# A two-layer attention and convolution kernel: the adaLN products placed anew in a hand-written order, and two norms that keep the squares of their last two tiles apart

## The chip, the cores and the metric

The kernel runs as one program on one NeuronCore of a Trainium2 chip. The metric is the device time of one execution in microseconds (us); lower is better.

## The reference, cut to what matters

Two layers work on 512 latent tokens of 1024 features. Layer 0 is a chunked gated linear attention (GLA) that also reads 256 context tokens; layer 1 is a Conformer convolution module. Each is followed by a SwiGLU feed-forward network (FFN), and each of the four sub-layers has an RMSNorm ahead of it that is scaled and shifted by a modulation (adaLN):

```
mod_lat = jax.nn.silu(c) @ w_mod[i] + b_mod[i]          # 6 vectors of 1024 for each layer
sh1, sc1, gt1, sh2, sc2, gt2 = jnp.split(mod_lat, 6)
h = modulate(rmsnorm(x, norm_mix_g[i]), sh1, sc1)       # y*(1+scale)+shift
x = x + gt1 * mixer(h)
x = x + gt2 * swiglu(modulate(rmsnorm(x, norm_ffn_g[i]), sh2, sc2), ...)
out = rmsnorm(x, final_norm_g)
```

`w_mod[i]` is a 1024 x 6144 matrix for each layer. An RMSNorm needs, for each token, the sum of the squares of its 1024 features.

## The kernel before, in words

Tokens lie along the free dimension and features along the 128 partitions, so the residual stream x is eight tiles `xs[0..7]` of 128 x 512. All projections run on TensorE (PE) as three matmuls on high and low parts of each number (`mm3`, lines 95 to 97; lines 369 to 371 for the values). The weights come by DMA from SyncE's queue (SP) into `wr`, ScalarE (ACT) casts them to a high part `wh` (L110), and VectorE (DVE) or GpSimd (POOL) subtracts to get the low part `wl` (L111).

The modulation vectors are not matmuls. `mod_jobs` (L217 to L238) is a generator: each step multiplies one 128 x 1024 tile of `w_mod` with the broadcast silu(c) on DVE and adds along the row ("product", L231), and only then asks for the DMA of the next tile (L223), because the tile `wm` has one buffer. `step(n)` takes n steps. The first step only loads. Products 1 to 24 (columns 16 to 39 of layer 0) are taken in the attention stage; `ffn(0, ...)` takes the later ones, two for each pair of hidden tiles.

The attention stage lies in a `manual_schedule` block: on PE, ACT, DVE and POOL the instructions run in the order in which the program writes them. That order is `plan` (L768): a list of projections ("fills"), and behind each the small stages that are run after it, by letters: `a` loads and splits coming weights, `o` copies the fill's result out, `m` is one product, `D`/`d` the decays of a head, `J`/`I` the masked scores (J scales queries and keys on DVE, L433/L434; I multiplies them on PE, L443), `X`/`y`/`x` the decays and transposes of the context's keys (y ends with L472 on DVE, x is L484 on PE), `S`, `K`, `T` states (T is L548 on DVE), `O`, `P`, `B`, `b` a head's output: O its matmuls (L560 to L562) and products with the gate (L573), P its mean square (L158 on PE, then eight small DVE operations L164 to L190), B the broadcast of the result on PE (L170), b its use (L586 to L590). `w304` and the like are parts of the output projection.

The plan holds 21 letters `m`; the line behind it takes the three that are left:

```
step(24 - sum(s_.split().count("m") for _, s_ in plan))
```

Outside the block a planner orders the instructions: it may take an instruction that comes later in the program into a time in which it believes the engine free. SP's order is always the planner's.

After the plan come the output projection `out_proj("wgo", ...)` in two token halves for its last two tiles (6 and 7), and `Norm.bc`. `Norm(7)` squares tiles 0 to 6 on ACT (L886) and adds them up on POOL (L888) in one accumulator; the square of tile 7 (L893) stays apart. Then `rstd_y` sums over the features with matmuls against a column of ones (L158), once for each of the two parts and each of two blocks of 128 tokens. There are four such norms: n1 behind the attention, n2 behind the first FFN, n3 behind the convolution, n4 at the end.

Of the kernel before, what the change touches and what calls it, by code (L numbers as in the profile page):

```python
# [55 lines left out]
def hybrid_kernel(ctx: ExitStack, tc: tile.TileContext, t: dict):  # L56
# [93 lines left out]
    def col(c, n=1):  # L150
        return cols[:, c:c + n]
# [62 lines left out]
    def make_a(dst, sc, g):  # L214
        dve.scalar_tensor_tensor(dst, sc, 1.0, g, op0=ALU.add, op1=ALU.mult)
# [378 lines left out]
    with tc.manual_schedule(engines=ENGS):  # L594
# [140 lines left out]
        d3 = dsum[:, 32:64].rearrange("p (k i two) -> p i k two", i=2, two=2)  # L735
# [8 lines left out]
        for k in range(KC):  # L744
            o = slice(k % 2 * CTX, (k % 2 + 1) * CTX)
# [3 lines left out]
        for k in range(KC + 1):  # L749
# [5 lines left out]
            if prev:  # L755
# [9 lines left out]

        plan = (("k2", "a D0 o d0 m"), ("g0", "o a"), ("kc0", "a o"), ("kc1", "o J0 a m"),  # L768
# [7 lines left out]
        names = [f for f, _ in plan] + ["w0", "w1", "w2", "w3"]  # L776
        head, parts = {}, {}

# [197 lines left out]
            nx.add(m, xs[m], c0, c1)  # L976
        return f

    n1, n2, n3, n4 = Norm(7), Norm(7), Norm(7), Norm(7)
    make_a(acol[:, 16:24], mod[0][:, 32:40], col(C_GFFN, 8))  # L980
    in1 = SubIn(n1, acol[:, 16:24], mod[0][:, 24:32])
    out_proj("wgo", KC, og, closing(mod[0][:, 16:24], n1), 6, in1, done={m: head[m][0] for m in head})
# [24 lines left out]
    D0, D7, A0, S1, S2, B7, G7 = 14, 13, 6, 12, 4, 20, 20  # L1007
# [550 lines left out]
```

## Time and profile before

| what | value |
|---|---|
| median of 3 runs | 1269.54 us (1267.61 to 1273.08) |
| the profiled execution's own time | 1270.32 us |
| its span from the first to the last instruction | 1268.5 us |
| mean granted TensorE clock | 0.984 of full speed |
| TensorE busy | 1231.4 us, 97% of the span |
| VectorE busy | 721.6 us, 57% |
| products on tile wm | 72 of 1206 to 3331 ns, median 1225 |

All stretches and starting times are microseconds from the start of the span. "Idle before" in a row of the timeline stands in brackets, with what ended it. The granted clock is 1.00 at 2.4 GHz and 0.50 at 1.2 GHz.

### The profile page before, as it was taken

The page shows a single profiled execution, that of the slowest core. Times are in us where ns is not written, and L with a number is a line of the kernel's source. Part 1 is how long each engine was busy: PE and PEld are TensorE (multiplying, and loading weights), DVE is VectorE, ACT ScalarE, POOL GpSimd, SP SyncE. Part 2 cuts the span into 40 slices and gives each one's busy share as a digit, 9 for nine tenths or more (in the row PEclk, how much of TensorE's full clock was granted, in tenths as well). Part 3 has the DMA queues.
Part 4 walks back from the last instruction along what each step waited for, and adds up shares of the span by engine and source line. Part 5 has one row for each costly group of instructions (what it writes and reads, how often), then busy time and mean ns, then how long its engine had stood idle before and what let it go on. Part 6 is the DMA issues. An engine that isn't in the chain of part 4 may idle for free.

```text
span 1268.5 us, 17022 instructions
## 1 busy us (share of the span) xinstructions
PE 1231.4 (97%) x6692; PEld 1068.6 (84%) x6692; DVE 721.6 (57%) x1289; ACT 476.1 (38%) x748; POOL 192.5 (15%) x154
## 2 busy tenths in 40 slices
PE   8899899999899999999999999999999999999997
PEld 7678799898798888888888988989988888888886
DVE  2997986755775555555323679986744333332223
ACT  3245655433342222222222469745522222232220
POOL 0033211112300000000011169913000000000110
PEclk7999999999899999999999999999999999999999
DMA  7742442323545656556333274422254333333322
GB/s 277 230 134 72 141 150 82 106 90 117 167 151 195 191 184 198 193 188 207 105 103 97 67 249 152 139 61 74 84 166 150 100 100 100 100 91 91 99 67 67
DMA packets 57780, 169.18 MB, mean 133 GB/s; under 512 B 6498, under 2 KB 12386, under 8 KB 57700
## 3 DMA queue, kind: packets, MB, share of 16 engines
q1 hardware_dynamic: 56036, 166.00, 40.8%
q10 hardware_dynamic: 1664, 2.10, 0.5%
q8 instruction: 52, 0.85, 0.3%
q14 instruction: 28, 0.23, 0.1%
HBM read 164.67 MB, written 3.41 MB: 132 GB/s over the span
## 4 chain that ended last, share of the span: by engine, by line
PE 77%; DVE 14%; issue 4%; ACT 3%; DMA 1%; POOL 1%; DVEq 0%; ACTq 0%; POOLq 0%
PE pm L95 22%; PE pm L96 22%; PE pm L97 22%; DVE g L256 3%; DVE pa L1096 2%; DVE wl L111 2%; PE pm L370 1%; PE pm L369 1%; PE pm L371 1%; DMA wm<-wmod 1%; ACT wh L110 1%; PE pa L623 1%; PE pm L530 1%; DVE pm L1096 1%; DVE t L276 1%
## 5 line engine op out<-in xcount | busy, mean ns | idle before, releaser
L110 ACT CAST wh<-wr 128x1024 fp32r<-128x1024 f32 (+2 forms) x197 | 200.4, 1025 | 484.1 <-PE pm L96 470.4
L97 PE MATMUL pm<-h,wl 128*128 128x512 f32 (+1 forms) x1008 | 372.0, 370 | 1.9 <-POOL wl L111 1.9
L96 PE MATMUL pm<-h,wh 128*128 128x512 f32 (+1 forms) x1008 | 371.0, 370 | 0.4 <-DVE h L199 0.4
L95 PE MATMUL pm<-h,wh 128*128 128x512 f32 (+1 forms) x1008 | 371.1, 371 | 0.2 <-ACT wh L110 0.2
L111 DVE TENSOR_TENSOR wl<-wr,wh 128x1024 fp32r<-128x1024 f32 (+1 forms) x176 | 221.1, 1260 | 244.7 <-ACT wh L110 242.8
L97 PEld LDWEIGHTS pm<-h,wl 128*128 128x128 f32 x1008 | 190.2, 189 | 35.1 <-POOL wl L111 2.8
L96 PEld LDWEIGHTS pm<-h,wh 128*128 128x128 f32 x1008 | 190.2, 189 | 32.2 <-DVE h L199 0.6
L95 PEld LDWEIGHTS pm<-h,wh 128*128 128x128 f32 x1008 | 189.3, 189 | 32.1 <-ACT wh L110 0.7
L95 PE MATMUL pm<-s,wh 128*128 128x512 f32 (+1 forms) x540 | 186.9, 346 | 1.1 <-ACT s L1276 1.1
L96 PE MATMUL pm<-s,wh 128*128 128x512 f32 (+1 forms) x540 | 186.0, 345 | 0.3 <-DVE s L281 0.2
L97 PE MATMUL pm<-s,wl 128*128 128x512 f32 (+1 forms) x540 | 185.5, 343 | 0.0
L231 DVE SCALAR_TENSOR_TENSOR wm<-wm,sil 128x1024 f32<-128x1024 f32 x72 | 93.9, 1304 | 108.4 <-DMA wm<-wmod 108.2
L888 POOL TENSOR_TENSOR g<-g,g 128x512 f32<-128x512 f32 (+1 forms) x31 | 39.9, 1288 | 748.3 <-ACT g L886 747.7
L96 PEld LDWEIGHTS pm<-s,wh 128*128 128x128 f32 x540 | 103.1, 191 | 13.2 <-DVE s L281 0.9
L95 PEld LDWEIGHTS pm<-s,wh 128*128 128x128 f32 x540 | 103.0, 191 | 13.1 <-ACT s L1276 1.3
L97 PEld LDWEIGHTS pm<-s,wl 128*128 128x128 f32 x540 | 102.9, 191 | 12.0
L111 POOL TENSOR_TENSOR wl<-wr,wh 128x1024 fp32r<-128x1024 f32 x21 | 52.6, 2517 | 215.4 <-ACT wh L110 200.6
L901 DVE SCALAR_TENSOR_TENSOR x<-pm,mod,x 128x256 f32<-128x256 f32 (+1 forms) x44 | 25.7, 600 | 52.6 <-PE pm L97 52.6
L1096 DVE SCALAR_TENSOR_TENSOR pa<-s,cols,pa 128x503 f32<-128x503 f32 (+18 forms) x80 | 52.8, 702 | 0.6
L369 PE MATMUL pm<-wh,h 128*128 128x256 f32 x128 | 37.0, 289 | 0.0
L371 PE MATMUL pm<-wl,h 128*128 128x256 f32 x128 | 36.2, 283 | 0.0
L370 PE MATMUL pm<-wh,h 128*128 128x256 f32 x128 | 36.2, 283 | 0.0
(267 smaller groups left out, 1511.2 us busy)
## 6 DMA issues: line engine op xcount, KB each, us to landing
wr<-wf SPq DMA_DIRECT2D x88, 512.0 KB, 4.3
wm<-wmod SPq DMA_DIRECT2D x72, 512.0 KB, 3.7
wr<-wo SPq DMA_DIRECT2D x32, 512.0 KB, 3.5
wr<-wp SPq DMA_DIRECT2D x24, 512.0 KB, 3.5
s<-toep SPq DMA_DIRECT2D x27, 256.0 KB, 5.4
s<-wmod SPq DMA_DIRECT2D x24, 256.0 KB, 5.1
wr<-wv SPq DMA_DIRECT2D x12, 512.0 KB, 3.8
wr<-wo SPq DMA_DIRECT2D x16, 384.0 KB, 3.2
```

Of the source, the lines that this page charges most:

```text
L95: pe.matmul(out, wh, xh, start=start, stop=False)
L96: pe.matmul(out, wh, xl, start=False, stop=False)
L97: pe.matmul(out, wl, xh, start=False, stop=stop)
L110: act.copy(hi[:, :n], raw[:, :n])
L111: lo_eng.tensor_tensor(lo[:, :n], raw[:, :n], hi[:, :n].bitcast(F32), op=ALU.subtract)
L231: dve.scalar_tensor_tensor(raw, raw, 1.0, sil, op0=ALU.mult, op1=ALU.mult, accum_out=dots[:, o:o + 1])
L256: dve.scalar_tensor_tensor(junk, wt, 1.0, vec, op0=ALU.mult, op1=ALU.mult, accum_out=dsum[:, o:o + 1])
L369: pe.matmul(o, a, wh[:, w], start=k == 0, stop=False)
L370: pe.matmul(o, b, wh[:, w], start=False, stop=False)
L371: pe.matmul(o, a, wl[:, w], start=False, stop=k == KC - 1)
L888: pool.tensor_tensor(self.acc[:, c0:c1], self.acc[:, c0:c1], s[:, c0:c1], op=ALU.add)
L1096: dve.scalar_tensor_tensor(p_[:, lo:hi], u_sb[m][:, lo + s:hi + s], wcol(m, j), p_[:, lo:hi], op0=ALU.mult, op1=ALU.add)
```

## The change

The plan gets three more letters `m`, 24 in all, so that the step behind it takes none. Four letters leave kc1, kc2, kc3 and vc2; seven are added at g0, kc0, vc1, va1, r6, vb3 and r7. The letters that stay keep their place among the other stages. Norms n1 and n3 become `Norm(6)`: the squares of tiles 6 and 7 both stay apart, and POOL no longer adds tile 6.

```diff
-        plan = (("k2", "a D0 o d0 m"), ("g0", "o a"), ("kc0", "a o"), ("kc1", "o J0 a m"),
-                ("k3", "a o Xa0 ya0"), ("kc2", "o a I0 m"), ("kc3", "a o Xa1 xa0 ya1 m"),
-                ("vc3", "a Xb0 o a xa1 yb0"), ("vc2", "xb0 m Xb1 o yb1 m a"), ("vc0", "o a xb1 D1 d1 m"),
-                ("va0", "o J1 S0 S3 K0 m"), ("vb0", "a o S2 I1 m"), ("vc1", "a o a T0 K1 m"),
-                ("va1", "o a D2 d2 S1 m"), ("vb1", "o J2 a O0 T1 m"), ("va2", "o a P0 m D3 O1 d3 J3"),
-                ("vb2", "o a I2 P1 m"), ("r5", "o a B0 K2 b0 B1 b1 m"), ("r6", "o a T2 I3 m"),
-                ("va3", "o a O2 K3 m a m"), ("vb3", "o P2 T3 m"),
-                ("r7", "o a B2 b2 w004 O3 m w104 P3 w204 B3 b3 m w304 w046 w146 w246 w346 w068 w168 w368 w268"))
+        plan = (("k2", "a D0 o d0 m"), ("g0", "o a m"), ("kc0", "a o m"), ("kc1", "o J0 a"),
+                ("k3", "a o Xa0 ya0"), ("kc2", "o a I0"), ("kc3", "a o Xa1 xa0 ya1"),
+                ("vc3", "a Xb0 o a xa1 yb0"), ("vc2", "xb0 Xb1 o yb1 m a"), ("vc0", "o a xb1 D1 d1 m"),
+                ("va0", "o J1 S0 S3 K0 m"), ("vb0", "a o S2 I1 m"), ("vc1", "a o a m T0 K1 m"),
+                ("va1", "o a m D2 d2 S1 m"), ("vb1", "o J2 a O0 T1 m"), ("va2", "o a P0 m D3 O1 d3 J3"),
+                ("vb2", "o a I2 P1 m"), ("r5", "o a B0 K2 b0 B1 b1 m"), ("r6", "o a m T2 I3 m"),
+                ("va3", "o a O2 K3 m a m"), ("vb3", "o m P2 T3 m"),
+                ("r7", "o a B2 b2 m w004 O3 m w104 P3 w204 B3 b3 m w304 w046 w146 w246 w346 w068 w168 w368 w268"))
...
-    n1, n2, n3, n4 = Norm(7), Norm(7), Norm(7), Norm(7)
+    n1, n2, n3, n4 = Norm(6), Norm(7), Norm(6), Norm(7)
```

## Rows read from the trace of the kernel before

**Rows 1.** The page: busy time of each engine, and the chain that ended last

```profile
PE 1231.4 (97%) x6692; PEld 1068.6 (84%) x6692; DVE 721.6 (57%) x1289; ACT 476.1 (38%) x748; POOL 192.5 (15%) x154
...
PE 77%; DVE 14%; issue 4%; ACT 3%; DMA 1%; POOL 1%; DVEq 0%; ACTq 0%; POOLq 0%
```

**Rows 2.** Waits of PE from 110 to 365: total us, times, longest

```profile
PE pm L484 <- DVE g L472: 3.6, 3, 1.5
PE pa L158 <- POOL g L888: 3.1, 2, 2.3
PE pm L170 <- DVE sm L190: 2.5, 1, 2.5
...
PE pa L158 <- ACT g L893: 0.9, 1, 0.9
```

**Rows 3.** Timeline of DVE from 112 to 245: start, duration, instruction, idle before

```profile
130.62 1.22 DVE L231 SCALAR_TENSOR_TENSOR wm<-wm,sil 128x1024 f32<-128x1024 f32 x1
...
136.61 0.68 DVE L434 TENSOR_TENSOR s<-s,s 128x512 f32<-128x512 f32 x1
...
151.96 3.33 DVE L231 SCALAR_TENSOR_TENSOR wm<-wm,sil 128x1024 f32<-128x1024 f32 x1 [0.72 <-DMA wm<-wmod]
```

**Rows 4.** Timeline of PE from 132 to 160

```profile
135.88 1.06 PE L443 MATMUL pa<-s,s 128*128 128x128 f32 x8
137.34 1.16 PE L443 MATMUL pa<-s,s 128*128 128x128 f32 x8 [0.40 <-DVE s L434]
...
158.96 1.01 PE L484 MATMUL pm<-ident,g 128*128 128x128 f32 x4 [1.48 <-DVE g L472]
```

**Rows 5.** Timeline of POOL from 100 to 420

```profile
133.68 2.46 POOL L111 TENSOR_TENSOR wl<-wr,wh 128x1024 fp32r<-128x1024 f32 x1 [9.53 <-ACT wh L110]
...
151.79 2.41 POOL L111 TENSOR_TENSOR wl<-wr,wh 128x1024 fp32r<-128x1024 f32 x1 [5.82 <-ACT wh L110]
...
297.38 1.29 POOL L574 TENSOR_TENSOR g<-g,g 128x512 f32<-128x512 f32 x1 [0.59 <-ACT g L570]
```

**Rows 6.** The tile wm over the whole span: its DMA from issue to landing

```profile
DMA to landing us min/median/max: 3.4/3.7/5.0
```

**Rows 7.** Windows: busy us of PE, PEld, DVE, ACT, POOL, clock, DMA share, GB/s

```profile
160.00:164.00 4.00, 4.00 (x23) 4.00 (x23) 2.73 (x9) 2.95 (x8) 0.00 (x0) 0.57 0.58 216
...
165.00:246.00 81.00, 81.00 (x617) 78.05 (x615) 57.03 (x126) 44.86 (x82) 15.68 (x7) 1.00 0.31 98
...
249.00:252.00 3.00, 3.00 (x12) 2.70 (x11) 2.32 (x5) 0.62 (x1) 0.00 (x0) 0.50 0.44 96
...
256.00:299.00 43.00, 43.00 (x305) 40.39 (x304) 23.36 (x45) 17.54 (x33) 12.66 (x6) 1.00 0.33 105
...
340.00:344.00 4.00, 4.00 (x20) 4.00 (x21) 1.30 (x8) 0.00 (x0) 0.00 (x0) 0.50 0.27 109
```

**Rows 8.** Timeline of DVE from 245 to 362

```profile
259.91 1.65 DVE L548 SCALAR_TENSOR_TENSOR t<-t,dec,pm 128x256 f32<-128x256 f32 x4
...
279.01 1.23 DVE L231 SCALAR_TENSOR_TENSOR wm<-wm,sil 128x1024 f32<-128x1024 f32 x1 [3.47 <-DMA wm<-wmod]
...
297.26 1.40 DVE L573 SCALAR_TENSOR_TENSOR d<-d,cols,pm 128x512 f32<-128x512 f32 x2
...
301.61 0.16 DVE L190 SCALAR_TENSOR_TENSOR sm<-sm,sm 128x4 f32<-128x4 f32 x1
...
331.52 1.23 DVE L231 SCALAR_TENSOR_TENSOR wm<-wm,sil 128x1024 f32<-128x1024 f32 x1 [2.00 <-DMA wm<-wmod]
```

**Rows 9.** Timeline of PE, from 245 to 304 and from 874 to 900

```profile
267.24 0.39 PE L562 MATMUL pm<-s,s 128*128 128x128 f32 x2
...
302.91 1.05 PE L170 MATMUL pm<-ident,sm 128*128 128x128 f32 x8
...
892.80 0.38 PE L158 MATMUL pa<-ones,g 128*128 128x1 f32 x2 [0.80 <-POOL g L888]
...
896.49 0.73 PE L158 MATMUL pa<-ones,g 128*128 128x1 f32 x6
```

## The prediction, on record before the changed kernel ran

> **What bounds the kernel now.** The page comes first: PE is busy for 97% of the span and holds 77% of the chain that ended last, DVE 14% [rows 1]. So an edit on DVE counts only where PE stands and waits for DVE, or where such a wait lowers PE's clock. The waits of PE in the attention stage and just behind it are therefore the second view. There are few: 3.6 us in three waits of the context's transposes for L472, 3.1 us and 0.9 us for the squares of norm n1, 2.5 us for a broadcast [rows 2]. The third view is the timeline around each. What the reader is to see there is that a product is seldom dear by its 1.2 us, but by what it waits for: the next tile is asked for only when the last product is done. A tile takes 3.7 us from issue to landing at the median, 3.4 to 5.0 [rows 6], and a product placed right behind another found its engine idle for 3.47 us [rows 8]. I call that the turnaround: 3.65 us of wait and 1.2 us of work. Everything queued behind a waiting product on DVE waits too.
>
> The fourth view is the granted clock. After waits of 1.5 and 1.48 us near 151 and 159, the stretch 160 to 164 ran at 0.57; after the 2.5 us wait that ended at 248.6, 249 to 252 ran at 0.50; after the waits of norm n1, 340 to 344 ran at 0.50, the lower of the two levels [rows 2, 4, 7]. A wait of about 2 us therefore costs about 1.5 us more: half of the 3 us that the row at 0.50 shows.
>
> **The front of the plan: g0 and kc0 take a product each; kc1, kc2, kc3 and vc2 lose one.** Before, product 1 runs at 130.62, then the gate's subtraction L287, and then J0, whose last operation ends at 137.29 [rows 3]. J0 feeds the two groups of L443 on PE: PE came to the first at 135.88 without a wait and to the second at 137.34 after 0.40 us [rows 4]. In the new order products 2 and 3 stand between L287 and J0.
>
> Product 2's tile is asked for at 131.85 and lands near 135.5. POOL has a subtraction from 133.68 to 136.14 [rows 5], and where product 4 met such a one (151.79 to 154.20) it ran 3.33 us, until 1.1 us behind POOL's end [rows 3, 5]; so product 2 ends at 136.14 + 1.1 = 137.25. Product 3's tile is asked for then: wait 3.7, work 1.15, end 142.1. J0's four operations at 0.61 end at 144.55. The second group of L443 moves from 137.34 to 144.65: PE is late by 7.3 us.
>
> What comes back: the products that left kc1, kc2 and kc3 make the three waits for L472 go away, 3.6 us [rows 2], since DVE, free of three products (one of them 3.33 us long behind a wait of 0.72 [rows 3]), reaches each L472 before a PE that is late by 7 us. The low clock of 160 to 164 goes with them: 0.43 of 4 us, 1.7 us [rows 7]. New is a low clock behind the wait of 7.5 us at 135.9: 1.2 to 2.8 us, by how much of the following 3 to 6 us runs at 0.50; I take 2.0. Sum: 7.3 - 3.6 - 1.7 + 2.0 = +4.0 us, with ends +2.0 (no new low clock) and +4.8. PE is busy for 81.00 of the 81 us from 165 to 246 [rows 7], so nothing there gives it back; the wait at 248.6 is on a chain that starts from PE and moves along.
>
> The Trainium skill (DMA: Bandwidth & Descriptors, Anatomy of one DMA) gives a transfer a fixed part of about 2.0 us and the rest at 436 GB/s; by that the 512 KB tile would take an estimated 3.2 us, and the front would cost 0.9 us less over its two tiles. The trace's 3.4 at the least speaks for the longer one. The Trainium skill (SBUF — State Buffer, Who interferes with whom) says that GpSimd and a VectorE instruction with two SBUF inputs exclude each other for the whole instruction; the 3.33 us product agrees.
>
> **The middle.** vc1 and va1 take a product each. PE is the bound there, and DVE works 57.03 of 81 us [rows 7] and stands idle ahead of both next stages, until PE or ACT has their inputs; the products end inside that idleness: nothing. Without it each would cost its 1.2 us. In r6 product 16 follows 15 directly, so T2, whose last four operations start at 259.91, comes 4.9 us later and ends near 266.6; the ACT scaling behind it ends by 267.1, and PE's first use is L562 at 267.24 [rows 8, 9]: 0 to 0.3 us, I take 0. If PE came there earlier, it would wait for all the rest.
>
> **vb3 and r7.** vb3's new product is a third in a row behind the one at 279.01, so P2 and T3 come 5 us later. PE has the fill of r7 between, 24 matmuls, and was busy for all 43 us from 256 to 299 [rows 7]; its next broadcast still comes behind P2's end, by about 1 us, so I take 0. r7's new product 22 stands behind b2, ahead of O3's two L573 at 297.26 [rows 8]; its tile is there. But product 23 follows those 1.4 us later, where its own old place had a landed tile: 297.3 + 1.2 for product 22, 3.65 for the tile with L573 inside it, 1.15 for product 23, so P3's small operations start at 303.4 and end at 304.9, in place of 301.77 [rows 8]. If POOL's L574 at 297.38 [rows 5] gets ahead of product 22, it is 1.3 us more. PE reaches B3 at 302.91 [rows 9]: a wait of 2.0 to 3.3 us that was not there, and with 0 to 1.7 us of low clock behind it 2.0 to 5.0; I take 4.2, since the wait is like the one at 248.6.
>
> **The three products that stood behind the plan.** They cost PE nothing where they stood: from 256 on PE has no wait [rows 7] until n1. What hurts is later. The product at 331.52, behind 2.00 us of idleness for its tile [rows 8], and a like one 5.6 us later belong to the FFN; the planner took them ahead, and they hold up the subtraction of the residual tiles 5 and 7. That is the 2.3 + 0.9 us of waits for n1's squares [rows 2] and the low clock to 344 [rows 7], half of the 6 us from 338: 6.2 together. The planner takes the next products as soon as a tile is free, so with the three gone it will take others into the same gaps: I take 0, with ends of -6.2 (none ahead of tiles 5 and 7) and +2 (one more late tile).
>
> **The norms.** POOL's adds of tile 6 go: PE waited for them 0.8 us at n1's second half (3.1 less 2.3) and 0.80 at n3's [rows 2, 9]. Against it, each half gets two matmuls more, which show as four records; six take 0.73 us [rows 9], so four take 0.48, or 1.9 over four halves. Net +0.3, with ends -1.6 and +1.9. At n1's first half PE waits for tile 7's square anyway.
>
> **Sum.** +4.0 + 4.2 + 0.3 = +8.5 on the profiled execution's 1270.3: 1278.8. The median lies 0.8 below that execution, so 1278. A measurement of this kernel can tell about 0.5%, 6.3 us, from no change: 1263.2 to 1275.9 counts as the same.
>
> **The rivals.** *The tail is relieved* (not slower): with DVE out of products when tiles 5 to 7 end, PE waits neither at 334 nor at 338 and keeps its clock, -6.2, so 1272. It decides from the point where no product with an unlanded tile stands ahead of the residuals of tiles 5 and 7. For it: these products follow the three in a chain, each asked for when the last was done. Against it: they are FFN products, and the planner has 48 more. Chance 0.20.
>
> *The loads are hidden*: J0 and P3 are not late, because the tiles land before DVE comes to them. Then the front gives 3.6 + 1.7 and r7 costs nothing: 1270.3 - 5.3 + 0.3 - 0.8 = 1264.5. Against it stands every pair of neighbouring products in the trace, 3.47 us idle [rows 8]. Chance 0.12; together with a relieved tail 1258, 0.06.
>
> *More waits*: the planner puts one product more ahead of a residual, and a longer low clock follows each wait: +5, 1283. Chance 0.12.
>
> My forecast has 0.50, between 1272 and 1281 by its ends (1269.5 + 2.0 + 2.0 - 1.6 and 1269.5 + 4.8 + 5.0 + 1.9). About 0.15 of it lies under 1275.9. Slower: 0.35 + 0.12 = 0.47. Same: 0.15, the tail's 0.19 and half of the hidden loads, 0.40 in all. Faster: the rest, 0.13. The range of 8 in 10 reaches from the hidden loads to past the added waits: 1264.5 to 1284.
>
> **What would show it.** Right: a wait of PE at L443 of about 7 us near 136, no waits at L484, 160 to 164 at full clock, a product idle some 3.7 us ahead of J0, a wait at L170 near 303 with a low clock behind it, products still ahead of the residuals near 330. Wrong: L443 without a wait (the front's sum falls by 8), L170 near 303 without one (r7's 4.2 falls), or no wait for n1's squares (the tail was relieved). At n3, L158 should wait for no POOL and be twelve records.

## The result, and the profile after

The changed kernel took 1277.07 us (median of 5 runs, 1274.51 to 1279.46), the kernel before 1267.61 (5 runs, 1266.43 to 1273.08). The ratio is 1.0076 [1.0049, 1.0102]: slower, with the whole interval above 1 and its lower end at about the half per cent that the prediction took for what a measurement can tell from no change. The prediction had 1278.

The page of the changed kernel gives busy times and the chain that ended last; against [rows 1], DVE and the loads of the modulation's tiles (DMA) hold more of the chain, PE less:

```profile
PE 1236.6 (97%) x6708; PEld 1073.5 (84%) x6708; DVE 717.8 (56%) x1289; ACT 475.6 (37%) x748; POOL 188.5 (15%) x150
...
PE 74%; DVE 15%; ACT 4%; issue 3%; DMA 3%; POOL 0%; DVEq 0%; ACTq 0%; POOLq 0%
```

The waits of PE from 110 to 375 (total us, times, longest) answer to [rows 2]. L484 has none any more; L443's has grown from 0.4, the wait for POOL's L574 is new, L170 has a second wait, and L158 waits for no L888:

```profile
PE pa L443 <- DVE s L434: 8.4, 1, 8.4
PE pm L170 <- DVE sm L190: 4.6, 2, 2.5
...
PE pm L158 <- POOL g L574: 1.2, 1, 1.2
PE pa L158 <- ACT g L893: 1.0, 1, 1.0
PE pm L562 <- ACT s L545: 0.2, 1, 0.2
```

DVE's timeline at the front (start, duration, instruction, idle before) answers to [rows 3]. Products 2 and 3 each wait for their tile, and J0's last operation ends at 148.45:

```profile
138.38 1.71 DVE L231 SCALAR_TENSOR_TENSOR wm<-wm,sil 128x1024 f32<-128x1024 f32 x1 [2.90 <-DMA wm<-wmod]
...
144.81 1.23 DVE L231 SCALAR_TENSOR_TENSOR wm<-wm,sil 128x1024 f32<-128x1024 f32 x1 [4.72 <-DMA wm<-wmod]
...
147.77 0.68 DVE L434 TENSOR_TENSOR s<-s,s 128x512 f32<-128x512 f32 x1
```

PE's timeline, answering to [rows 4, 9]: the wait at the front, the first of four L484 without one, r6's L562, the two waits in r7, and n3's second half:

```profile
147.30 3.79 PE L443 MATMUL pa<-s,s 128*128 128x128 f32 x16 [8.35 <-DVE s L434]
...
154.67 0.60 PE L484 MATMUL pm<-ident,g 128*128 128x128 f32 x4
...
274.05 0.49 PE L562 MATMUL pm<-s,s 128*128 128x128 f32 x2 [0.18 <-ACT s L545]
...
307.51 1.05 PE L158 MATMUL pm<-ones,g 128*128 128x1 f32 x8 [1.20 <-POOL g L574]
...
315.14 1.16 PE L170 MATMUL pm<-ident,sm 128*128 128x128 f32 x8 [2.13 <-DVE sm L190]
...
901.12 0.50 PE L158 MATMUL pa<-ones,g 128*128 128x1 f32 x4
...
904.92 0.95 PE L158 MATMUL pa<-ones,g 128*128 128x1 f32 x8
```

Windows (columns as in [rows 7], the granted clock third from the end) behind these waits. The clock is 0.50, its lower level, or between the two, behind each of the three:

```profile
147.30:151.00 3.70, 3.70 (x17) 3.70 (x18) 3.63 (x7) 0.20 (x1) 0.00 (x0) 0.50 0.54 143
151.00:155.00 4.00, 4.00 (x31) 4.00 (x31) 2.32 (x6) 2.78 (x6) 1.43 (x1) 0.82 0.31 119
...
309.00:313.00 4.00, 4.00 (x11) 2.68 (x9) 1.47 (x3) 0.00 (x0) 0.00 (x0) 0.57 0.37 131
...
316.00:319.00 3.00, 3.00 (x10) 2.38 (x9) 1.93 (x3) 0.62 (x1) 0.00 (x0) 0.54 0.12 49
```

Two profiled executions can't be laid over each other from zero. Their openings differ although the work up to product 1 is the same: 32 small matmuls took 4.18 us in the kernel before and 6.97 in the changed one. At the context's gate, L390, which stands behind product 1 in both and waits 1.58 and 1.57 us, PE was at 132.70 before and at 135.62 after. PE's rows of before, then of after:

```profile
10.15 4.18 PE L623 MATMUL pa<-ones,s 128*128 128x1 f32 x32
...
132.70 0.47 PE L390 MATMUL pm<-s,d 128*128 128x256 f32 x2 [1.58 <-DVE s L287]
```

```profile
10.47 6.97 PE L623 MATMUL pa<-ones,s 128*128 128x1 f32 x32
...
135.62 0.47 PE L390 MATMUL pm<-s,d 128*128 128x256 f32 x2 [1.57 <-DVE s L287]
```

So I take off that difference, 2.92 us here, and call what is left the **shift** at a point: how much later than before a kernel is there, counted from the gate. The three points are the broadcast that started at 248.60 before (behind the front and the middle), B3's L170 at 302.91 (behind r7) and the broadcast of n1's second half at 358.66 (behind the tail). The changed kernel's shifts are +3.8, +9.3 and +6.3; n3's second half stands at 902.08 and 910.60, +5.6, and the spans, 1268.5 and 1277.6, end at +6.2. So the front costs 3.8, the stretch of vb3 and r7 5.5 (called r7's below), the tail gives back 3.0, and n3 0.7.

The table holds every run, with the ratio of its times to those of the kernel before beside it. The medians lie higher than the shifts at n1's end say, by 2.0 us in the mean over the 13 rows (from 1.6 lower to 5.6 higher): the profiled execution of before, 1270.32, is itself 2.7 above the median of its five runs, and a shift comes from one execution of each kernel. Shifts compare places within a kernel and kernels with each other; the ratios are the verdicts.

| kernel | ratio, 95% interval | shift at 248.6 | at B3 | at n1's end |
|---|---|---|---|---|
| the change | 1.0076 [1.0049, 1.0102] | +3.8 | +9.3 | +6.3 |
| front alone | 1.0046 [1.0032, 1.0060] | +3.6 | +3.5 | +3.2 |
| back alone | 1.0049 [1.0036, 1.0062] | 0.0 | +5.2 | +7.3 |
| norms alone | 0.9983 [0.9965, 1.0000] | 0.0 | 0.0 | -0.8 |
| the change, old norms | 1.0091 [1.0071, 1.0112] | +3.7 | +8.8 | +8.1 |
| one product ahead of J0 | 1.0029 [1.0012, 1.0046] | -2.7 | +2.7 | -0.3 |
| tiles 2, 3 not loaded | 1.0020 [1.0006, 1.0034] | -2.7 | +2.8 | -1.2 |
| tiles 16, 20, 22, 23 not loaded | 1.0042 [1.0024, 1.0060] | +3.9 | +4.5 | +3.1 |
| vb3 as before | 1.0049 [1.0032, 1.0066] | +3.8 | +6.3 | +5.6 |
| r7's first product gone | 1.0041 [1.0018, 1.0065] | +4.0 | +6.8 | +6.2 |
| only the harmless moves | 0.9985 [0.9967, 1.0004] | -5.0 | -6.2 | -7.2 |
| three products into the middle | 1.0046 [1.0026, 1.0066] | +6.5 | +6.9 | +3.9 |
| harmless moves and a gate | 0.9933 [0.9909, 0.9957] | -5.0 | -6.2 | -12.3 |

### The profile page after: what moved, and what is told of

Same layout as the page of the kernel before. It is cut to its first block, busy times and chain, and to the rows that moved or that the text cites. A ratio compares the mean times of both kernels' runs of the same rounds, so it can differ in the third digit from the quotient of the medians.

```text
span 1277.6 us, 17061 instructions
## 1 busy us (share of the span) xinstructions
PE 1236.6 (97%) x6708; PEld 1073.5 (84%) x6708; DVE 717.8 (56%) x1289; ACT 475.6 (37%) x748; POOL 188.5 (15%) x150
## 4 chain that ended last, share of the span: by engine, by line
PE 74%; DVE 15%; ACT 4%; issue 3%; DMA 3%; POOL 0%; DVEq 0%; ACTq 0%; POOLq 0%
PE pm L95 22%; PE pm L96 22%; PE pm L97 22%; DVE g L256 3%; DMA wm<-wmod 2%; DVE pa L1096 2%; DVE wl L111 2%; DVE wm L231 2%; ACT wh L110 1%; PE pa L623 1%; PE pm L370 1%; PE pm L371 1%; PE pm L369 1%; DVE pm L1096 1%; DVE t L276 1%
## 5 line engine op out<-in xcount | busy, mean ns | idle before, releaser
L888 POOL TENSOR_TENSOR g<-g,g 128x512 f32<-128x512 f32 (+1 forms) x27 | 35.6, 1317 | 752.6 <-ACT g L886 752.1
L901 DVE SCALAR_TENSOR_TENSOR x<-pm,mod,x 128x256 f32<-128x256 f32 (+1 forms) x44 | 25.6, 601 | 55.4 <-PE pm L97 55.4
```

Source lines behind the costliest of these rows:

```text
L888: pool.tensor_tensor(self.acc[:, c0:c1], self.acc[:, c0:c1], s[:, c0:c1], op=ALU.add)
```

## The experiments

**The change in four parts.** The first run had only the moves at the front and in the middle, the second only r6, vb3 and r7 (and so nothing behind the plan), the third only the norms, the fourth all that the trace of after spoke for.

```
front alone (against before)
  g0 "o a m"  kc0 "a o m"  kc1 "o J0 a"  kc2 "o a I0"  kc3 "a o Xa1 xa0 ya1"
  vc2 "xb0 Xb1 o yb1 m a"  vc1 "a o a m T0 K1 m"  va1 "o a m D2 d2 S1 m"
back alone (against before)
  r6 "o a m T2 I3 m"  vb3 "o m P2 T3 m"  r7 "o a B2 b2 m w004 O3 m ..."
norms alone (against before)
- n1, n2, n3, n4 = Norm(7), Norm(7), Norm(7), Norm(7)
+ n1, n2, n3, n4 = Norm(6), Norm(7), Norm(6), Norm(7)
only the harmless moves (against the change)
  g0 "o a"  kc0 "a o"  r6 "o a T2 I3 m m"  vb3 "o P2 T3 m m"  r7 "o a B2 b2 w004 O3 m ..."
```

> Only the letters of g0, kc0, kc1, kc2, kc3, vc2, vc1 and va1 move; r6, vb3, r7 and the norms stay as before, and three products are left for the end. Theory (a product right behind another holds DVE for the turnaround of its tile): PE waits some 8 us at the second group of L443, none at L484, and the sum is +3.8 us, ratio 1.003. Rival (the front gives back all it takes, and the loss is made in r7): ratio 1.000.

> Only the letters of r6, vb3 and r7 are added; the front and the norms stay as before, and none is left for the end. Theory: PE waits some 3 us near P3 and B3 with a low clock behind it, +5.5, and the waits behind the output projection are shorter by 3: +2.5 us in all, ratio 1.002. Rival (all of the change's loss comes from here): +9.5, ratio 1.0076. Rival (taking the three from the end is a gain that outweighs r7): below 0.998.

> Only n1 and n3 keep the squares of tiles 6 and 7 apart. Theory: no wait of L158 for POOL any more (0.8 us each at n1's and n3's second half), four records more in each half, 0.5 us: between -1 and +1 us, ratio 0.999 to 1.001. Rival (the sums at full price): +1.9.

> The letters leave kc1, kc2, kc3 and vc2 as in the change, but none goes to g0 and kc0; the places in vc1 and va1 stay; r6 and vb3 take their second product at their very end, r7 is as before, three are left for the end; norms as changed. Theory: the three waits at L484 and the low clock of 160 to 164 go, 5.3 us, nothing new in the front or at B3: 1262, ratio 0.996. Rival (a product costs PE its time wherever it stands): ratio 1.000 or more.

The front alone and the back alone are each slower, by 0.46% and 0.49%; the norms alone are 0.17% faster, with an interval that ends at no change. The three add up to 0.78%, the whole has 0.76%. With the norms alone PE still waited 1.2 us for POOL at n1, where I had expected no such wait. The back alone shows the waits of r7 without any front, and that a plan with nothing left behind its end doesn't relieve the tail: PE still waits for n1's squares (PE, back alone), and the shift grows from +5.2 to +7.3 there, where I had expected +2.5 at the end.

```profile
304.78 2.08 PE L170 MATMUL pm<-ident,sm 128*128 128x128 f32 x8 [3.66 <-DVE sm L190]
...
341.58 0.52 PE L158 MATMUL pa<-ones,g 128*128 128x1 f32 x2 [2.49 <-POOL g L902]
```

(In a kernel whose plan has a line for each stage, L888 is L902 and L893 is L907.) Taking the products away from kc1, kc2, kc3 and vc2, with none put ahead of J0, is worth 5.0 us of shift by itself: the rows of the harmless moves. Their ratio, 0.9985, doesn't tell them from no change, where I had expected 0.996.

Their further step from -5.0 to -6.2 at B3 fits the clock and not a product. The wait at 248.6 is 2.51 or 2.52 us in the change, in both kernels with the harmless moves and in the run with one product ahead of J0 (below). Behind it the clock was 0.58 in the changed kernel, and 1.00 in the other three. Windows of the change and of the run with one product:

```profile
255.30:258.80 3.50, 3.49 (x13) 3.19 (x14) 2.82 (x6) 0.62 (x1) 0.00 (x0) 0.58 0.42 95
```

```profile
244.50:248.00 3.50, 3.45 (x19) 3.05 (x20) 2.81 (x5) 0.62 (x1) 0.00 (x0) 1.00 0.40 94
```

**What of a product makes J0 late.** Two runs at the front, both against the change. In the first, products 2 and 3 multiply the landed tile again; in the second, kc0's product is gone.

```
tiles 2, 3 not loaded
- if n + 1 < len(ij) and ij[n + 1] < (1, 40):
+ if n + 1 < len(ij) and ij[n + 1] < (1, 40) and n + 2 not in (2, 3):
one product ahead of J0
- ("kc0", "a o m")
+ ("kc0", "a o")
```

> The changed kernel, but products 2 and 3 load no tile of their own: they multiply the tile of product 1 again, so three columns of the modulation are computed from the wrong weights. DVE does as much work as before this edit, in the same order; only the turnaround of two tiles is gone. Theory (J0 is late because of the two waits for a tile, 2.9 and 4.7 us): those two waits vanish, PE's wait at L443 falls from 8.4 to 1 to 2.5 us, the position of the first output's B-part and of everything behind it comes 5 to 7.5 us earlier than in the changed kernel, and the time is 0.998 to 1.003 of the kernel before. Rival (it is DVE's own work, or POOL's subtraction beside it, that makes J0 late): L443 still waits over 5 us and the time stays at 1.006 to 1.008.

> The changed kernel without the product in kc0: one product (number 2) stands between product 1 and J0 in place of two, and one product goes behind the plan. Theory (each product on the way to J0 costs one turnaround and its own work, 3.7 + 1.2 us): PE's wait at L443 is 8.4 - 4.9 = 3.5 us, and everything behind it comes 4.5 to 6 us earlier than in the changed kernel; 1.002 to 1.005 of the kernel before. Rival (there is slack ahead of J0 that one product fits into, and only the second one costs): the wait is under 1 us and the time 0.997 to 1.001.

Without the two loads DVE does the same work, and L443 waits 2.39 us in place of 8.35; all behind comes 6.4 us earlier (+3.8 to -2.7), within the theory's 5 to 7.5. It is the turnaround. What is left of the wait is DVE's work, and most of it product 3's, which ran 3.33 us beside POOL's subtraction (130.66 to 133.06 in this run). DVE, then PE, of the run without the loads:

```profile
130.82 3.33 DVE L231 SCALAR_TENSOR_TENSOR wm<-wm,sil 128x1024 f32<-128x1024 f32 x1
```

```profile
135.41 2.82 PE L443 MATMUL pa<-s,s 128*128 128x128 f32 x16 [2.39 <-DVE s L434]
```

With one product the wait was 2.38, not the 3.5 of the theory and not the rival's under 1: the first product costs 2.0 over the old 0.40, the second 6.0. The reason is in the rows. DVE waits 3.04 us for product 2's tile while POOL subtracts (132.32 to 134.72); in the kernel before, J0's own third operation met that subtraction and took 2.89 us at 133.79, the three others 0.68 or 0.69. The first turnaround covers a loss that J0 had anyway; the second finds nothing to cover.

```profile
134.23 1.57 DVE L231 SCALAR_TENSOR_TENSOR wm<-wm,sil 128x1024 f32<-128x1024 f32 x1 [3.04 <-DMA wm<-wmod]
```

**What makes B3 late.** Three runs against the change: four loads at the back left out as above, `n + 2 not in (16, 20, 22, 23)`; vb3 as before, `"o P2 T3 m"`; r7 without its first product, `"o a B2 b2 w004 O3 m ..."`.

> The changed kernel, but products 16, 20, 22 and 23 load no tile of their own and multiply the tile of the product before them again (four columns of the modulation are computed from the wrong weights). Theory (the turnaround is the cost in r7 as well): the 1.2 us that the broadcast waits for POOL's L574 and the 2.1 us wait of B3 with the low clock behind them go; from 320 on all comes 4 to 6 us earlier than in the changed kernel, L443 still waits 8 us, and the time is 1.002 to 1.005. Rival (three products in vb3 and r7 are too much work for DVE there, tiles or not): B3 still waits 1.5 us or more, and the time stays at 1.006 to 1.008.

> The changed kernel with vb3 as it was before (its first product removed, one product goes behind the plan); r7 keeps its new product behind b2. Theory (the products of vb3 make T3 late, T3 holds up ACT's casts and with them POOL's L574, for which the broadcast of P3 waits; the pair in r7 makes P3's own chain late): the 1.2 us wait of L158 for POOL's L574 near 307 goes, and the 2.1 us wait of L170 stays, at 2 to 3.7 us, as the run with the back alone showed it (3.7). The time is 1.005 to 1.009. Rival (vb3's late end is what makes both late): both waits go and the time falls to 1.001 to 1.004.

> The changed kernel without r7's first product (one product goes behind the plan). Theory (B3's wait of 2.1 us is the turnaround between the products before and behind O3; the 1.2 us wait of L158 for POOL's L574 is vb3's): the wait of L170 near 315 and the low clock behind it go, the wait for L574 stays between 0.8 and 1.5 us, B3 comes 4 to 5.5 us earlier than in the changed kernel, of which the tail may take back up to 3; time 1.003 to 1.006. Rival (the wait of B3 comes from L574 being late, whatever products stand there): both waits stay, time 1.006 to 1.008.

Without the loads r7 costs +0.5 (3.9 to 4.5) in place of 5.5: again the turnaround, not DVE's work. The other two split it. With vb3 as before, the wait for L574 fell to 0.27 and the one of L170 to 1.78 (PE):

```profile
303.50 1.05 PE L158 MATMUL pm<-ones,g 128*128 128x1 f32 x8 [0.27 <-POOL g L574]
...
309.18 1.16 PE L170 MATMUL pm<-ident,sm 128*128 128x128 f32 x8 [1.78 <-DVE sm L190]
...
343.08 0.38 PE L158 MATMUL pa<-ones,g 128*128 128x1 f32 x2 [2.36 <-ACT g L893]
```

Without r7's first product the wait for L574 stayed and the one of L170 went (PE):

```profile
301.82 1.05 PE L158 MATMUL pm<-ones,g 128*128 128x1 f32 x8 [1.25 <-POOL g L574]
...
306.73 1.50 PE L170 MATMUL pm<-ident,sm 128*128 128x128 f32 x8
...
340.70 0.38 PE L158 MATMUL pa<-ones,g 128*128 128x1 f32 x2 [2.10 <-ACT g L893]
```

So vb3's third product is the one wait and r7's pair the other, as the theory had it, though the 1.78 is a little under its 2, and B3 came only 2.5 us forward in the last run and not 4 to 5.5. Undoing vb3's product brings B3 3.0 us forward and undoing r7's 2.5, together the 5.5 of the whole. The way of the first, by the trace of the change: products in a row hold T3, ACT's scalings of T3 wait for it, and the casts queued behind them come at 297.19; POOL's three subtractions of those casts stand ahead of L574, which starts at 305.89 where it was 297.38 before [rows 5], 5.6 us later counted from the gate. POOL's rows:

```profile
298.30 7.49 POOL L111 TENSOR_TENSOR wl<-wr,wh 128x1024 fp32r<-128x1024 f32 x3 [16.95 <-ACT wh L110]
305.89 1.56 POOL L574 TENSOR_TENSOR g<-g,g 128x512 f32<-128x512 f32 x1
```

What I had not expected stands in the table: each of these two edits brings B3 2.5 to 3.0 us forward, and n1's end only 0.1 to 0.7. PE comes to n1 earlier and waits longer there: 2.36 and 2.10 us in place of 1.03. Its bound at that place is the last residual, not B3; and that stands, on DVE, behind a product that waited 1.97 and 1.95 us for its tile. Both runs leave one product behind the plan, which the change doesn't, so they can't tell how much of the loss is that product's.

**The norms in the change.**

```
- n1, n2, n3, n4 = Norm(6), Norm(7), Norm(6), Norm(7)
+ n1, n2, n3, n4 = Norm(7), Norm(7), Norm(7), Norm(7)
```

> The changed kernel with all four norms as before (only tile 7's square kept apart); the new order of the products stays. Run by itself, the norms' edit had brought n1's last broadcast 1.4 us forward. Theory (in the changed kernel POOL's add of tile 6 would come later still, because the products ahead of the residual tiles come later; keeping it apart is what recovers the 3 us between the first output's B-part and n1's end): PE waits 2 to 3 us for POOL's L888 at n1 again, n1's end comes 3 to 5 us later than in the changed kernel, and the time is 1.009 to 1.013. Rival (the edit of the norms is worth the same here as by itself, and the 3 us come from the products that no longer stand behind the plan): n1's end comes 0.5 to 1.5 us later, and the time is 1.007 to 1.009.

PE waits for POOL's add again (PE, below), n1's end is 1.8 us later, and the tail gives 0.7 in place of 3.0. That lies between theory and rival: the norms' edit is worth more here than the 0.8 it had by itself, but less than 3. The interval of the ratio, [1.0071, 1.0112], holds both.

```profile
346.24 0.38 PE L158 MATMUL pa<-ones,g 128*128 128x1 f32 x2 [2.78 <-POOL g L888]
```

**A version for all this, first try.** The harmless moves, and the three products behind the plan put as second ones at va0, vb0 and vb1.

```
  va0 "o J1 S0 S3 K0 m m"  vb0 "a o S2 I1 m m"  vb1 "o J2 a O0 T1 m m"
```

> All that the runs so far speak for: no product between product 1 and J0, none taken from r6, vb3 and r7 ahead of their stages' own work, the two norms with two tiles apart, and the three products that stood behind the plan as second products at the ends of va0, vb0 and vb1, where DVE was seen idle. Theory (these three places are free, the front gives back 4.9 us, nothing waits in r7, and with no product behind the plan the tail gives 1 to 3 us): no wait at L443, L484 or L170 but the 2.5 us one that every kernel has; n1's end 7 to 10 us earlier than before; time 0.993 to 0.998. Rival (a second product in the middle delays PE as it did at the front): new waits of PE between 165 and 246, and 0.998 to 1.003.

The rival's mechanism was right, and the time, 1.0046, is above even its 0.998 to 1.003: PE was busy for 73.69 of the 81 us from 165 to 246, where it had been busy for all of them [rows 7]. DVE's idleness there is not free for a pair: five products stand on it from 176.65 to 197.8, each behind its tile and with little between them; L548 comes late behind them, ACT waits 10.35 us for it, and PE 5.71 us for ACT. DVE, ACT and PE of this run:

```profile
191.66 1.23 DVE L231 SCALAR_TENSOR_TENSOR wm<-wm,sil 128x1024 f32<-128x1024 f32 x1 [3.93 <-DMA wm<-wmod]
...
196.61 1.23 DVE L231 SCALAR_TENSOR_TENSOR wm<-wm,sil 128x1024 f32<-128x1024 f32 x1 [3.72 <-DMA wm<-wmod]
```

```profile
198.47 1.71 ACT L545 ACTIVATE s<-t,dec 128x256 f32<-128x256 f32 x4 [10.35 <-DVE t L548]
```

```profile
201.39 1.22 PE L390 MATMUL pa<-s,d 128*128 128x512 f32 x2 [5.71 <-ACT s L519]
```

**Second try: keep products away from the last residuals.** The harmless moves with their three products behind the plan, and an added dependence, called a gate here, on all later ones: they multiply by a 1 made from tile 7's first half, so none of them can be taken ahead of it.

```
- dve.scalar_tensor_tensor(raw, raw, 1.0, sil, ...)
+ dve.scalar_tensor_tensor(raw, raw, one1 if n >= 24 else 1.0, sil, ...)
...
          nx.add(m, xs[m], c0, c1)
+         if nx is n1 and m == KC - 1 and c0 == 0:
+             dve.tensor_scalar(one1, xs[m][:, 0:1], 0.0, 1.0, op0=ALU.mult, op1=ALU.add)
```

> The kernel with the moved products only where they cost nothing (products taken from kc1, kc2, kc3 and vc2, none put ahead of J0, r7 as before, three products behind the plan, two tiles apart in n1 and n3), and beside that the products of the FFN made to wait for the first half of residual tile 7: they multiply by a 1 that DVE computes from that tile, so the planner can't take them ahead of it. Theory (products with an unlanded tile ahead of the residuals of tiles 5 and 7 make the waits for n1's squares): PE's waits of 1.7 and 0.4 us near 333 fall to 0.5 us in all and the low clock behind them goes; n1's end comes 2 to 5 us earlier than in the same kernel without the gate, which had it 7.2 us earlier than before; the time is 0.992 to 0.997. Rival (the waits come from the last tiles' own squares, or the products only move to a place where they cost as much): n1's end stays within 1.5 us of the kernel without the gate, and the time is 0.997 to 1.000.

It took 1258.59 us (1254.73 to 1261.94) against 1268.24: 0.9933 [0.9909, 0.9957], faster than both kernels, and the interval lies below that of the harmless moves without the gate. Without the gate PE waited twice at n1 and ran at 0.58 and 0.57 behind it (PE, then windows, of the harmless moves):

```profile
332.88 0.61 PE L158 MATMUL pa<-ones,g 128*128 128x1 f32 x4 [1.73 <-POOL g L902]
...
335.74 1.86 PE L158 MATMUL pa<-ones,g 128*128 128x1 f32 x8 [0.38 <-ACT g L907]
```

```profile
333.00:337.00 4.00, 3.62 (x19) 3.33 (x20) 1.63 (x3) 0.42 (x1) 0.00 (x0) 0.58 0.66 198
337.00:341.00 4.00, 4.00 (x22) 4.00 (x23) 1.29 (x8) 0.00 (x0) 0.00 (x0) 0.57 0.16 65
```

With it PE waits for nothing from 300 to 375, and the clock stays at 1.00. The first gated product follows tile 7's residual (DVE, then one of the windows):

```profile
325.28 0.48 DVE L916 SCALAR_TENSOR_TENSOR x<-pm,mod,x 128x256 f32<-128x256 f32 x1 [2.40 <-PE pm L97]
325.80 0.15 DVE L993 TENSOR_SCALAR one<-x 128x1 f32<-128x1 f32 x1
325.99 1.28 DVE L232 SCALAR_TENSOR_TENSOR wm<-wm,one,sil 128x1024 f32<-128x1024 f32 x1
```

```profile
327.00:331.00 4.00, 4.00 (x34) 3.91 (x35) 2.53 (x12) 1.36 (x2) 0.00 (x0) 1.00 0.46 133
```

B3 stands where it stood without the gate (-6.2 in both), n1's end 5.1 us earlier. The two waits (2.1) and the low clock (0.42 and 0.43 of 4 us, 3.4) are 5.5.

## Why the prediction was right, and where it was not

**The front: right in sign, cause and size.** Predicted +4.0, measured +3.8. J0 was to be late by 7.3; the wait at L443 is 8.35 in place of 0.40 (it stands ahead of the first group, not the second), mostly because DVE waited 4.72 us for product 3's tile where 3.7 was counted. The waits at L484 went, 3.6, and the low clock of 160 to 164 with them, 1.7. The new low clock is 0.50 of 3.7 us and 0.18 of 4, 2.6, inside its bounds of 1.2 to 2.8. One term was missing: behind each old wait the four transposes took 1.01 us, and the same three groups now take 0.60, 0.60 and 0.91, 0.9 less together. 7.95 - 3.6 - 1.7 + 2.6 - 0.9 is 4.35, half a microsecond more than the shift. The Trainium skill (DMA: Bandwidth & Descriptors, Anatomy of one DMA), by which a tile would take an estimated 3.2 us, gives its figures for transfers that GpSimd issues, and SyncE issues these; it would have made the front cheaper, and the 4.72 speaks against it. The Trainium skill (SBUF — State Buffer, Who interferes with whom) has a GpSimd instruction that reads SBUF and a VectorE instruction with two SBUF inputs exclude each other; the trace agrees, with 3.33 us in the run without the loads and with the 2.89 us of J0's own operation before.

**The middle and r6: right.** The shift is +3.8 at the fourth L484 (167.31 before, 174.02 after) and +3.8 at 248.6: vc1's and va1's products cost nothing. L562 waits 0.18, within the 0 to 0.3. How narrow that is shows in the run with one product ahead of J0: there the clock stayed at 1.00 behind the wait at 248.6, PE came to L562 earlier, and it waited 1.41 us. The pairs of the first try show the same for the middle.

**vb3 and r7: the wait was foreseen, its cost and one of its two causes were not.** B3's wait of 2.13 lies in the 2.0 to 3.3. The step that failed is vb3's 0: it looked at P2's broadcast alone. T3, late as well, holds ACT's casts and so POOL's L574, which I had only thought of as getting ahead of product 22. That is 1.20 us of wait and a low clock of its own at 309. The two cost 5.5 by the shift in place of 4.2, and not as they were counted: by the undoing, vb3's 0 is 3.0 and r7's 4.2 is 2.5.

**The tail: the term that failed most.** I counted r7's 4.2 through to the end, and nothing back. 3.0 came back ahead of n1's second half. In the rows it is that PE waits 1.03 us for tile 7's square where before it waited 2.30 and 0.85 at n1's first half, and that the low clock of 340 to 344 [rows 7] is not there (346 to 350 at 1.00). PE's rows of before, then of after:

```profile
336.53 0.38 PE L158 MATMUL pa<-ones,g 128*128 128x1 f32 x2 [2.30 <-POOL g L888]
...
339.32 1.44 PE L158 MATMUL pa<-ones,g 128*128 128x1 f32 x6 [0.85 <-ACT g L893]
```

```profile
349.32 0.38 PE L158 MATMUL pa<-ones,g 128*128 128x1 f32 x2 [1.03 <-ACT g L893]
```

Undoing shows that 1.8 of it hangs on the norms' edit. That the rest comes from a PE which arrives later and so waits less is argued, and no run shows it alone. The planner took FFN products into the tail's gaps as I had said; with nothing behind the plan they still stood ahead of the last residuals (L901, which adds to the residual; the prediction calls it a subtraction). The price of those products, 6.2 by the prediction, was measured with the gate at 5.1, on top of the harmless moves. So the rival of a relieved tail had its mechanism right, and this change did not bring it about.

**The norms: wrong in sign.** +0.3 was predicted, with -1.6 as the lower end. n1 gained 0.8 by itself and 1.8 within the change, n3 0.7 (from +6.3 to +5.6): 1.5 by itself, near that end, and 2.5 within the change, beyond it. n3's second half shows no wait for POOL and twelve records, as said. The added records cost 0.34 us there where 0.48 was counted.

**The sum.** 8.5 was predicted; the trace shows 6.2 from the gate on. By the medians it is 9.5, by the ratio's interval between 6.2 and 12.9. That the profiled executions differ by 9.1 is for 2.9 the opening, in which nothing was changed. r7 was counted 1.3 too low and the tail with the norms some 4 too high, so by the shifts the sum was 2.3 too high; the median lies 3.3 above the shift's 6.2. That 1277.07 came so near to 1278 is thus in part luck. The signs of the two large terms and their mechanism, the turnaround of the one tile, are what the runs bear out.

Open: why the opening runs at two speeds, and whether one kernel meets the longer one more often than another; why the clock fell behind the wait at 248.6 in some profiles and not in others; and why the harmless moves are worth 7 us by the shift and no certain gain by the ratio.

## What to carry to other kernels

Work that was thought of as filler for an idle engine cost its turnaround here, not its duration: with one buffer, ask of each place what stands queued behind the load, and never put two pieces in a row ahead of something that the bounding engine needs. Follow a late stage through every engine that it feeds, to the last one queued behind: vb3's lateness reached PE by ACT's casts and POOL. And a loss ahead of a place where PE waits anyway is partly free, just as a gain ahead of it is partly lost: before mending one wait, look at the next one, and take away the last in the row first. Here that was worth 5.1 us on top of the harmless moves.

## What the runs showed of the hardware

An opening that is the same in all kernels has two speeds: the first 32 matmuls of L623 took 3.81 to 4.33 us in nine of the fourteen profiles and 6.96 or 6.97 in five, and the place of the context's gate varied from 127.74 to 135.78. In the run with one product ahead of J0 the granted clock reads 0.50 over the 6.96 us; in the changed kernel it reads 1.00 over 6.97, so the record of the clock doesn't fit the matmuls there.

A wait was sometimes followed by a stretch at the lower clock and sometimes not. In the kernel before, 1.48 us near 159 was (0.57 from 160 to 164) and 1.51 near 151 was not (1.00 from 152 to 156); in the changed kernel 1.20 us at 307.51 was (0.57 from 309 to 313) and 1.03 at n1 was not (1.00 from 346 to 350). The same wait of 2.51 or 2.52 us for L190 near 248.6 was followed by 0.52 before, by 0.58 in the change, and by 1.00 in three other kernels. So what a wait costs beyond its own length, which the prediction put at about 1.5 us for one of 2, is not the same in each execution.
